# A logsumexp kernel without its check on the sums and without the branch that the check decides

## The chip, the cores and the metric

The kernel runs on one core of a Trainium2 chip. Its engines work side by side, each through its own list of instructions, and wait for each other on semaphores: ScalarE (ACT) computes functions such as exp and Ln, VectorE (DVE) sums, TensorE (PE) multiplies matrices, SyncE (SP) issues the transfers (DMAs) between the chip's main memory and the on-chip memory, and GpSimd (POOL) does nothing here but set constants at the start. The metric is the device time of one execution in microseconds (us).

## The reference

```python
def reference(x, axis):            # x: 32 x 512 x 1024 float32, normally distributed; axis = -1
    x_max = np.max(x, axis=axis, keepdims=True)
    return (x_max.squeeze(axis) + np.log(np.sum(np.exp(x - x_max), axis=axis))).astype(np.float32)
```

For each of 16,384 rows of 1024 numbers it gives the logarithm of the sum of the exponentials. The input has 67.1 MB, the output 64 KB.

## The kernel before

The 16,384 rows are spread over the 128 partitions, 128 rows on each. The kernel computes exp without subtracting the row's maximum first, sums, and takes the Ln. That is right as long as the sums stay in a safe range, so this version looks at the sums afterwards, and a branch leads to a second computation, with the maximum subtracted, where one of them is outside it.

The 128 rows of a partition come in 17 chunks (`CHUNKS`), of 4 to 16 rows at the start and in the middle, and 5, 4, 3, 2, 1, 1, 1, 1 at the end. SP loads each chunk with one DMA into a ring of 51 rows (line 119), and waits before it until the rows that stood there have been used. ACT waits for the chunk's landing. For the first rows of a chunk (second number in `CHUNKS`) it computes exp in place (line 163), and DVE sums them (line 183, or in halves, line 170). For the other rows, all of the last four chunks among them, ACT adds up while it computes exp, by means of its accumulator, which a separate read instruction stores (line 190). The sums of the last four rows go to a tensor of their own, `late`, the others to `sums`.

`take_logs` (line 123) is the Ln of a stretch of rows into `res` (line 127). It is called three times: for 81 rows when the chunk with index 7 (`LN_AT`) comes, for the 43 rows that follow directly behind the last exp, and for the last four rows. SP then waits for the last Ln and issues the output's DMA (line 232).

The check on the sums has these steps. `count` (line 200) compares sums with a lowest and a highest value and adds up how many lie inside, twice per call, on DVE (line 204): once for the 124 sums of `sums`, once for the 4 of `late`, after the last Ln. PE multiplies the counts by `ones` and so adds over the partitions (line 226), DVE adds the four results into one whole number, `n_good` (line 229). SP, ACT and DVE each wait for it, load it into a register (line 236) and branch (line 274): if it is not 2 x 128 x 128, they carry out the second computation (lines 241 to 273), and otherwise jump behind it. In the second computation ACT has 8 x 16 exps and one Ln, DVE 8 maxima, 8 sign changes and an addition, SP 8 loads and a store.

At the end SP waits until all three engines have loaded the register (line 277), clears the semaphores (line 278), takes `known` back to zero (line 279), and waits for the landing of the output, `stored` (line 280), which it takes back too (line 281).

## Time and profile before

| what | value |
|---|---|
| time, median of 3 runs | 165.16 us (165.04 to 165.38) |
| time of the profiled execution | 165.16 us |
| span of the profiled execution | 161.5 us, 171 instructions |
| input and output over the span | 67.18 MB, 416 GB/s on average |
| DVE busy | 122.1 us (76% of the span), of it 111.2 us sums on line 183 |
| ACT busy | 115.1 us (71%), of it 104.4 us exps on line 163 |
| PE busy | 0.2 us |

The span goes from the kernel's first instruction to its last; what the runtime does ahead of it and behind it is not in it, but the time contains some of that. A line of a view that tells of instructions names the source line (L163), the engine, the operation, what is written from what (`ring<-ring`) and how often. SPq, ACTq and DVEq are the engines' sequencers, which wait, branch, load registers and issue DMAs. In the chain that ended last, each piece is what released the next one. In a table of windows a row holds the stretch in us from the span's start, its length, the busy time of PE, weight loads, DVE, ACT and POOL with the number of instructions, the TensorE clock that was granted, the busy share of the DMA engines, and GB/s.

### The profile page before, as it was taken

How to read it: one execution, taken by the hardware profiler on the slowest of the kernel's cores; microseconds unless marked ns; L12 is line 12 of the kernel's file. 1: busy time of each engine (PE TensorE's matmuls, PEld its weight loads, DVE VectorE, ACT ScalarE, POOL GpSimd, SP SyncE). 2: the span in 40 equal slices, each digit the busy share in tenths (PEclk: the TensorE clock that was granted, in tenths of full speed). 3: DMA queues.
4: the chain of work that ended last, by engine and by line, in shares of the span. 5: the costliest groups of instructions: out<-in, count | busy, mean ns of one | idle time of the engine just before them, and what ended most of it. 6: DMA issues, size and time to landing. Idle time of an engine off the chain costs nothing.

```text
span 161.5 us, 171 instructions
## 1 busy us (share of the span) xinstructions
PE 0.2 (0%) x2; PEld 0.1 (0%) x2; DVE 122.1 (76%) x56; ACT 115.1 (71%) x40; POOL 0.2 (0%) x4
## 2 busy tenths in 40 slices
PE   0000000000000000000000000000000000000000
PEld 0000000000000000000000000000000000000000
DVE  0028000003999999999999599999999999999894
ACT  3170005996079960999419993999199999999995
POOL 0000000000000000000000000000000000000000
DMA  7999899979979979979979999999999999999990
GB/s 272 491 487 426 365 426 520 438 341 520 438 341 520 438 341 520 438 341 520 438 309 455 455 455 438 422 422 422 412 429 429 422 440 395 452 402 439 402 396 27
DMA packets 2593, 67.18 MB, mean 416 GB/s; under 512 B 288, under 2 KB 416, under 8 KB 928
## 3 DMA queue, kind: packets, MB, share of 16 engines
q1 hardware_dynamic: 2592, 67.18, 97.2%
q14 instruction: 1, 0.01, 0.0%
HBM read 67.11 MB, written 0.07 MB: 416 GB/s over the span
## 4 chain that ended last, share of the span: by engine, by line
DMA 48%; DVE 30%; ACT 20%; issue 1%; PE 0%; ACTq 0%
DMA ring<-in_x_dram 48%; DVE sums L183 29%; ACT ring L163 17%; ACT ring L190 3%; DVE marks L204 0%; ACT res L127 0%; PE good L226 0%; DVE n_good L229 0%; ACTq L126 0%
## 5 line engine op out<-in xcount | busy, mean ns | idle before, releaser
L183 DVE TENSOR_REDUCE sums<-ring 128x8 f32<-128x8192 f32 (+5 forms) x14 | 111.2, 7994 | 35.6 <-ACT ring L163 35.6
L163 ACT ACTIVATE ring<-ring 128x8192 f32<-128x8192 f32 (+6 forms) x18 | 104.4, 5836 | 43.2 <-DMA ring<-in_x_dram 43.1
L170 DVE CUSTOM_DVE_ANT_0 ring<-ring 128x512 f32<-128x512 f32 x16 | 9.9, 689 | 0.0
L190 ACT ACTIVATE ring<-ring 128x1024 f32<-128x1024 f32 x9 | 9.3, 1044 | 0.0
L150 ACT ACT_TABLE_LOAD x1 | 1.3, 1283 | 1.4 <-PEq L89 1.4
L190 ACT ACTIVATION_READ_ACCUMULATOR ring<-ring 128x1 f32 x9 | 1.6, 173 | 0.0
L170 DVE DVE_READ_ACCUMULATOR2_ANT sums<- 128x1 f32 x16 | 1.4, 85 | 0.0
L149 DVE MEMSET ones<- 128x1 f32 x1 | 0.1, 59 | 1.5 <-PEq L89 1.5
L204 DVE TENSOR_SCALAR_CACHE_REDUCE marks<-late 128x4 f32<-128x4 f32 x2 | 0.3, 190 | 0.9 <-ACT res L127 0.9
L204 DVE TENSOR_SCALAR_CACHE_REDUCE marks<-sums 128x124 f32<-128x124 f32 x2 | 0.5, 309 | 0.0
L127 ACT ACTIVATE res<-sums 128x81 f32<-128x81 f32 (+1 forms) x2 | 0.5, 242 | 0.0
L226 PE MATMUL good<-counts,ones 128*1 128x4 f32 x2 | 0.2, 166 | 160.1 <-DVE marks L204 160.1
L229 DVE TENSOR_REDUCE n_good<-good 1x1 int32<-1x4 f32 x1 | 0.1, 148 | 0.3 <-PE good L226 0.3
L204 DVE DVE_READ_ACCUMULATOR marks<-sums 128x1 f32 x2 | 0.3, 142 | 0.0
L204 DVE DVE_READ_ACCUMULATOR marks<-late 128x1 f32 x2 | 0.3, 163 | 0.0
L127 ACT ACTIVATE res<-late 128x4 f32<-128x4 f32 x1 | 0.2, 173 | 0.0
L226 PEld LDWEIGHTS good<-counts,ones 128*1 128x1 f32 x2 | 0.1, 80 | 160.1 <-DVE marks L204 160.1
L309 POOL MEMSET const-uint8-127<- 128x1 uint8 x1 | 0.1, 102 | 0.0
L309 POOL MEMSET const-bfloat16-1.0<- 128x1 bf16 x1 | 0.1, 101 | 0.0
L309 POOL MEMSET const-float32-0.0<- 128x1 f32 x1 | 0.1, 98 | 0.2 <-issue 0.2
L309 POOL MEMSET const-float32-1.0<- 128x1 f32 x1 | 0.1, 98 | 0.0
## 6 DMA issues: line engine op xcount, KB each, us to landing
ring<-in_x_dram SPq DMA_DIRECT2D x1, 7680.0 KB, 24.4
ring<-in_x_dram SPq DMA_DIRECT2D x1, 7168.0 KB, 28.7
ring<-in_x_dram SPq DMA_DIRECT2D x1, 6656.0 KB, 35.8
ring<-in_x_dram SPq DMA_DIRECT2D x1, 4608.0 KB, 20.3
ring<-in_x_dram SPq DMA_DIRECT2D x2, 2048.0 KB, 16.1
ring<-in_x_dram SPq DMA_DIRECT2D x1, 3584.0 KB, 28.4
ring<-in_x_dram SPq DMA_DIRECT2D x1, 2560.0 KB, 27.3
ring<-in_x_dram SPq DMA_DIRECT2D x4, 512.0 KB, 27.0
```

The lines of the kernel that those rows point to most:

```text
L127: nc.scalar.activation(out=res[:, lo:hi], in_=src, func=Ln).then_inc(act_done, 1)
L149: check(nc.vector.memset(ones, 1.0))
L150: nc.scalar.preload_act_table_set("natural_log_exp_and_others")
L163: nc.scalar.activation(out=ring[:, s + lo : s + hi], in_=ring[:, s + lo : s + hi], func=Exp).then_inc(act_done, 1)
L170: nc.vector.tensor_tensor_reduce(out=ring[:, s + j, : D // 2], in0=ring[:, s + j, : D // 2], in1=ring[:, s + j, D // 2 :], scale=1.0, scal ...
L183: nc.vector.reduce_sum(out=sums[:, row + lo : row + hi], in_=ring[:, s + lo : s + hi], axis=AX).then_inc(dve_done, 1)
L190: nc.scalar.activation(out=ring[:, s + j], in_=ring[:, s + j], func=Exp, accum_out=total(row + j),).then_inc(act_done, 1)
L204: nc.vector.tensor_scalar(out=marks[:, c * NB + at : c * NB + at + n], in0=src, scalar1=bound, scalar2=None, op0=op, op1=Op.add, accum_out ...
L226: check(nc.tensor.matmul(good[:1, :4], lhsT=ones, rhs=counts, start=True, stop=True))
L229: nc.vector.reduce_sum(out=n_good, in_=good[:1, :4], axis=AX).then_inc(known, 1)
L309: nc = _bacc.Bacc("TRN2", target_bir_lowering=False, num_devices=1)
```

## The change

The check on the sums goes, and with it the branch and the second computation: the counts, the matrix product, the number `n_good`, the three register loads, and all semaphores that belong to them. The three calls of `take_logs` and the output's DMA stay, in their order. At the end SP clears the semaphores as soon as it has issued the output's DMA, and waits for the landing after that.

```diff
-    top, low, total_g, res_g = (ring[:, STEP, k * NB : (k + 1) * NB] for k in range(4))
...
-    check(nc.vector.memset(ones, 1.0))
     nc.scalar.preload_act_table_set("natural_log_exp_and_others")
...
-    def count(src, k, at):
-        ...
-    nc.vector.wait_ge(dve_done, dves)
-    nc.vector.wait_ge(act_done, done_before[-1 - LATE][1])
-    count(sums[:, :late_row], 0, 0)
     last_sum = acts
 
     take_logs(logged, late_row, sums[:, logged:late_row], *done_before[-1 - LATE])
     take_logs(late_row, NB, late[:, : NB - late_row], dves, last_sum)
-    nc.vector.wait_ge(act_done, acts)
-    count(late[:, : NB - late_row], 1, late_row)
-    nc.tensor.wait_ge(checked, checks)
-    check(nc.tensor.matmul(good[:1, :4], lhsT=ones, rhs=counts, start=True, stop=True))
-    nc.vector.wait_ge(checked, checks)
-    with nc.allow_low_precision(reason="small whole numbers"):
-        nc.vector.reduce_sum(out=n_good, in_=good[:1, :4], axis=AX).then_inc(known, 1)
-
     nc.sync.wait_ge(act_done, acts)
     nc.sync.dma_start(out=out_v, in_=res).then_inc(stored, 16)
 
-    for engine, reg in ((nc.sync, E.SP), (nc.scalar, E.Activation), (nc.vector, E.DVE)):
-        engine.wait_ge(known, 1)
-        engine.reg_load(deciders[reg], n_good)
-        engine.sem_inc(known, 1)
-
-    with nc.If_ne(deciders, 2 * P * NB):
-        ...
-    nc.end_ifs()
-
-    nc.sync.wait_ge(known, 4)
     nc.sync.sem_clear(range(used[0], used[-1] + 1))
-    nc.sync.sem_inc(known, -4)
     nc.sync.wait_ge(stored, 16)
     nc.sync.sem_inc(stored, -16)
```

## The prediction

> **What bounds the kernel now.** I read the page's chain first, then the end of the span in the timeline, then what ends each wait on the output's path, and last the windows behind the span, because the change touches only what comes after the last sum. The page and its chain:

> ```profile
> span 161.5 us, 171 instructions
> ## 4 chain that ended last, share of the span: by engine, by line
> DMA 48%; DVE 30%; ACT 20%; issue 1%; PE 0%; ACTq 0%
> DMA ring<-in_x_dram 48%; DVE sums L183 29%; ACT ring L163 17%; ACT ring L190 3%; DVE marks L204 0%; ACT res L127 0%; PE good L226 0%; DVE n_good L229 0%; ACTq L126 0%
> ```

> Up to the last exp the bound is the input stream, with exps and sums in step with it. The change leaves all of that alone. It can earn something only where the chain has L204, L226 and L229: after the last Ln. The chain in order of time, its end:

> ```profile
> 155.37 3.02 ACT ring L190 x7
> ...
> 159.48 0.21 ACT res L127 x2
> 159.70 0.02 issue
> 159.72 0.37 DVE marks L204 x4
> 160.09 0.04 issue
> 160.13 0.21 PE good L226 x2
> 160.34 0.02 issue
> 160.36 0.15 DVE n_good L229
> ```

> ACT is done at 159.69 us. From there two strands run side by side: the output's DMA on SP, and the count, matmul, sum, register loads and branch. The timeline, the DMA issues and the answers for tile n_good and line 274 show both:

> ```profile
> 159.71 0.35 SPq L232 DMA_DIRECT2D out_dram<-res  x1
> ```

> ```profile
> out_dram<-res SPq DMA_DIRECT2D x1, 64.0 KB, 1.5
> ```

> ```profile
> L236 SPq TENSOR_LOAD <-n_good x1: 461/461/461, 160.5 to 160.5; - x1
> L236 ACTq TENSOR_LOAD <-n_good x1: 461/461/461, 160.5 to 160.5; - x1
> L236 DVEq TENSOR_LOAD <-n_good x1: 540/540/540, 160.5 to 160.5; - x1
> ```

> ```profile
> L274 SPq COMPARE_BRANCH  x1: 45/45/45, 161.1 to 161.1; - x1
> L274 ACTq COMPARE_BRANCH  x1: 45/45/45, 161.1 to 161.1; - x1
> L274 DVEq COMPARE_BRANCH  x1: 72/72/72, 161.2 to 161.2; - x1
> ```

> The output is issued at 159.71 and its last receipt arrives 1.5 us later (161.26 in the trace's semaphore records). The branches end at 161.1 to 161.2. So the whole check on the sums lies beside the output's flight and sticks out by little. After the branch SP still clears semaphores and updates two more (lines 278, 279, 281, in a row, about 0.08 us apart), and the span ends at 161.45.

> **Behind the span.** The execution took 165.16 us (the median of the runs is the same number), its span 161.45: 3.71 us lie around the span. The trace goes on after it. The windows there:

> ```profile
> 161.50:161.90 0.40, 0.00 (x0) 0.00 (x0) 0.00 (x0) 0.00 (x0) 0.00 (x0) 1.00 0.00 0
> 161.90:162.60 0.70, 0.00 (x0) 0.00 (x0) 0.00 (x0) 0.00 (x0) 0.00 (x0) 1.00 0.05 12
> 162.60:164.20 1.60, 0.00 (x0) 0.00 (x0) 0.00 (x0) 0.00 (x0) 0.00 (x0) 1.00 0.00 0
> 164.20:164.70 0.50, 0.00 (x0) 0.00 (x0) 0.00 (x0) 0.00 (x0) 0.00 (x0) 1.00 0.04 16
> ```

> The last two numbers are the DMA share and GB/s: in a time without kernel work one transfer appears, 12 GB/s for 0.7 us, some 8 KB. In the DMA records it is one 8192-byte packet of the instruction queue, from 161.975 to 162.506, that is 0.87 us after ACT's branch ended. The semaphore records tell the rest. Semaphore 2, which the kernel does not own, is updated at 160.497, which is 0.16 us after PE's last matmul reported (160.336), and then eight more times, at 163.809, .847, .891, .915 up to 164.131. Then some 250 semaphores are cleared until 164.70, and a second such round of semaphore 2 runs from 164.92 to 165.28. I read the rounds as a meeting of the five engines, one after another: PE arrives first, the second arrives at 163.81, and the others, already there, follow within some 0.04 us each. That second engine kept everybody waiting for 2.4 us after SP's end. POOL had nothing to do since 1.4 us, so it is one of the three that branch. Of these ACT skips most: the fallback has 8 x 16 exps and a Ln for it, 129 instructions, against 8 x 2 + 1 on DVE and 8 loads, a store and a few semaphore steps on SP. So I take it that ACT, having jumped, had to fetch its next instructions, and the end of the execution waited for that.

> **The change part by part.**
> Removed on DVE: `ones`' memset (0.06 us at 1.5 us; ACT's first exp waits for data until 7.43, so nothing); the count over 124 sums (158.21 to 158.80, beside the last exp, with nothing queued on DVE that the output needs): nothing. The count over the last 4, the matmul, the sum and the loads of the register run from 159.72 to 161.09, beside the output's flight to 161.26: nothing by themselves. If the output landed sooner than 161.1, they would have been the end; it does not.
> Removed on SP, behind the output's issue: wait for the count, register load, branch, wait for the other two. `sem_clear` now follows the issue directly and is over by about 160.2, hidden by the flight. Left behind the landing: the wait for `stored` and its update, 0.017 us, which reports at 161.453 at present, 0.19 us after the last receipt. It will be at 161.26 + 0.04 = 161.30. **Span: 161.45 - 0.15 = 161.30 us.**
> Both Ln calls and the output's issue stay where they are: the diff does not touch `take_logs`, so no part of the change comes from the Ln.
> Removed behind the span: the three jumps. ACT ends its program at 159.70 and goes straight on, DVE at 158.2. If the fetch after the jump is what the meeting waited for, the last to arrive is SP. In the kernel before the fifth hop, the last of the way forth and so by the order of arrival SP's at the latest, is at 163.915. What SP needs from its last instruction to the meeting is not shown, since it is hidden behind 163.81. Bounds: PE's 0.16 us from one side, and from the other 1.30 us, the time from the end of the fetched packet (162.51) to the late arrival (163.81), which may be plain end-of-program work. I take PE's row, since it alone is an engine that went on without a jump. Then SP arrives at 161.30 + 0.16 = 161.46 in place of 163.915: **2.46 us less, 165.16 - 2.46 = 162.70 us**; with 1.30 it is 162.60, 1.32 us less, 163.84. The span's 0.15 us is contained in both. The meeting can't be earlier than 161.3, so the time goes no lower than about 162.55, and the runs' own scatter (165.04 to 165.38) takes it to 162.45.

> [...] The row: a packet of instructions 0.87 us after the branch, and an engine late by 2.4 us. [...]

> **The rivals.**
> *Only the span shrinks, 165.0 us.* Either the late arrival isn't the jump's doing (the end of any program takes that long on ACT or SP), or the 3.71 us lie ahead of the span: the semaphore records also show a round at -3.82 to -2.39 us. Against the first: PE passes in 0.16 us, and the packet comes just after the branch. Against the second: the closing round ends at 165.28, close to 165.16. If it holds, the price is 165.16 - 0.15 = 165.01. A chance of 0.17.
> *The fetch moves to SP, slower.* [...] If SP, the last to finish, has to fetch at its end, it pays there what the late engine pays now: from 161.105 (branch) to 163.81, 2.70 us, so it arrives at 161.30 + 2.70 = 164.00 in place of 163.915, about 165.25. A second fetch of 0.87 us behind it makes 166.1. It decides against the change from a delay of 2.95 us on (163.915 + 0.33 - 161.30). [...] A chance of 0.06.

> **How the numbers follow.** What a measurement of this kernel can tell from no change is about 0.2%, 0.33 us. The meeting comes early: 0.77, by itself 162.45 to 163.85, likeliest 162.70. Only the span: 0.17, 164.85 to 165.2. Slower: 0.06. All of the first is faster by over 0.2%, all of the second within. To leave out no more than 2 in 10 the range takes in the second case: 162.45 to 165.10.

> **What would show it.** A span of 161.30, with the output's issue at 159.71 and its landing 1.5 us later as before; no L204, L226, L229, L236, L274. Behind the span: no 8 KB of instructions within 1.5 us of ACT's end, and the eight updates of semaphore 2 beginning at 161.5 or before. If the fetch is gone and the meeting still waits until about 163.7, the closing code itself takes that long and the first rival holds. If the meeting comes early and the time stays, the 3.71 us are ahead of the span. If the output lands later or the last exp ends after 159.5, the difference comes from the input stream, and this prediction has missed its place.

## The result, and the profile after

The changed kernel takes 162.59 us (median of 6 runs, 162.49 to 162.74) against 165.16 us (164.62 to 165.41) for the kernel before: a ratio of 0.9846, with a 95% interval of 0.983 to 0.9863. The forecast was 162.70 us, in a range from 162.45 to 165.10. Its profiled execution took 162.59 us, of which the span is 161.27. So 0.18 us of the 2.57 are inside the span, and the rest behind it: what lies around the span (the time less the span) went from 3.71 us to 1.32.

The head of the page, the chain and the chain's end in order of time, after:

```profile
span 161.3 us, 149 instructions
## 4 chain that ended last, share of the span: by engine, by line
DMA 48%; DVE 29%; ACT 20%; issue 1%; ACTq 0%
DMA ring<-in_x_dram 48%; DVE sums L154 29%; ACT ring L134 17%; ACT ring L161 3%; ACT res L107 0%; ACTq L106 0%
```

```profile
159.30 0.15 ACT ring L161
159.45 0.20 ACT res L107 x2
```

Up to the last Ln the chain is what it was; L204, L226 and L229 are gone from it, and nothing has taken their place. Line numbers have shifted (L107 is the Ln of `take_logs`, L176 the output's issue). The timeline's and the DMA issues' lines of the output:

```profile
159.68 0.35 SPq L176 DMA_DIRECT2D out_dram<-res  x1
```

```profile
out_dram<-res SPq DMA_DIRECT2D x1, 64.0 KB, 1.6
```

The windows behind the span, of the kernel after (no PE columns here, since PE has no work):

```profile
161.50:161.90 0.40, 0.00 (x0) 0.00 (x0) 0.00 (x0) 1.00 0.00 0
161.90:162.60 0.70, 0.00 (x0) 0.00 (x0) 0.00 (x0) 1.00 0.00 0
162.60:164.20 1.60, 0.00 (x0) 0.00 (x0) 0.00 (x0) 1.00 0.00 0
```

The 12 GB/s that stood in the second of these windows are gone. The trace's records of semaphore 2, which show where the five engines meet behind the program, in us from the span's start:

| | first (PE) | second | third | fourth | fifth | ninth | second round ends |
|---|---|---|---|---|---|---|---|
| before | 160.497 | 163.809 | 163.847 | 163.891 | 163.915 | 164.131 | 165.279 |
| after | 1.654 | 159.770 | 159.808 | 159.852 | 161.410 | 161.573 | 162.717 |

Read together the rows name the engines. PE, without work in the kernel after, comes at 1.65. The second follows ACT's last Ln (159.66) by 0.11 us, so it is ACT. The fifth follows SP's last instruction (161.268) by 0.14 us, so it is SP, and it is now the one that the others wait for.

### The profile page after: what moved, and what is told of

It is laid out like the page before. It is cut to its first block, busy times and chain, and to the rows that moved or that the text cites. A ratio compares the mean times of both kernels' runs of the same rounds, so it can differ in the third digit from the quotient of the medians.

```text
span 161.3 us, 149 instructions
## 1 busy us (share of the span) xinstructions
DVE 121.0 (75%) x46; ACT 115.0 (71%) x40; POOL 0.2 (0%) x4
## 4 chain that ended last, share of the span: by engine, by line
DMA 48%; DVE 29%; ACT 20%; issue 1%; ACTq 0%
DMA ring<-in_x_dram 48%; DVE sums L154 29%; ACT ring L134 17%; ACT ring L161 3%; ACT res L107 0%; ACTq L106 0%
## 5 line engine op out<-in xcount | busy, mean ns | idle before, releaser
L107 ACT ACTIVATE res<-sums 128x81 f32<-128x81 f32 (+1 forms) x2 | 0.5, 242 | 0.0
L107 ACT ACTIVATE res<-late 128x4 f32<-128x4 f32 x1 | 0.2, 173 | 0.0
```

The source lines that it names most:

```text
L107: nc.scalar.activation(out=res[:, lo:hi], in_=src, func=Ln).then_inc(act_done, 1)
```

## The experiments

In the kernel before, ACT's branch jumps over 128 exps with accumulator and a Ln, its part of the second computation. The theory: ACT's jump over them waits for instructions, and the meeting waits for ACT. The readings are, for each run, the end of ACT's branch, the second update of semaphore 2, the time between them, and the first 8192-byte packet of the instruction queue behind the branch, in us, all from its profiled execution, and then the device time. A time marked * is the median of 4 runs or more, any other is a single run. The kernel before was timed again beside the experiments: 165.05 us with e1 to e4, 164.97 with e5 to e8, 165.22 with e9 to e11, 164.63 with e12; the ratios below are to these runs.

| kernel | branch ends | second update | between | packet | time |
|---|---|---|---|---|---|
| before | 161.105 | 163.809 | 2.70 | 161.975 | 165.16* |
| after | none | 159.770 | | none | 162.59* |
| e1, no branch | none | 160.680 | | none | 162.62* |
| e2, ACT skips 1 exp a step | 161.376 | 161.915 | 0.54 | 162.362 | 163.09* |
| e5, 4 exps a step | 160.833 | 161.377 | 0.54 | 162.059 | 162.73 |
| e6, 8 exps a step | 161.015 | 161.559 | 0.54 | 162.005 | 162.92 |
| e7, 12 exps a step | 161.361 | 164.165 | 2.80 | 162.240 | 165.52 |
| e9, 8 a step, 64 exps added far ahead | 160.811 | 161.354 | 0.54 | 161.797 | 162.71 |
| e12, 12 a step, 64 exps added far ahead | 161.158 | 161.701 | 0.54 | 162.141 | 163.01* |
| e3, ACT alone jumps | 161.604 | 164.179 | 2.58 | 162.476 | 165.02* |
| e4, whole guard, wide exps | 161.253 | 161.462 | 0.21 | 162.887 | 163.05* |
| e8, the same, early clear | 160.927 | 161.131 | 0.20 | 162.579 | 163.01* |

The profiled executions fall into groups by what lies around the span, too: 1.32 to 1.33 us in the kernel after, e1 and e10, where no jump stands at the end; 1.56 in e2, e5, e6, e9 and e12; 3.71 to 3.82 in the kernel before, e3 and e7. (e4 and e8, with 1.56 and 1.54, have another ending, told below.)

**e1: the checks without the branch.**

```diff
-    with nc.If_ne(deciders, 2 * P * NB):
-        ...
-    nc.end_ifs()
```

> The kernel before with the branch and the second computation left out; counts, matrix product, n_good, the three register loads and the wait for all three stay. Theory (ACT's jump over the second computation waits for instructions): no jump, so semaphore 2's second update comes right behind ACT's register load, at about 161.1, and the fifth follows SP's end by 0.14 us as in the kernel after; with SP's end at 161.35 to 161.45 the time is 162.65 to 162.8. Rival A (any taken branch costs it): the same. Rival B (the checks themselves, the loads of n_good from on-chip memory above all, make ACT late): second update still near 163.8, 165.2 us.

It took 162.62 us, a ratio to the kernel before of 0.9856 (0.9839 to 0.9872), and the counts, the matrix product and the sum cost nothing that can be measured (the kernel after takes 162.59). They are still at the end of its chain:

```profile
159.69 0.37 DVE marks L204 x4
160.06 0.04 issue
160.10 0.21 PE good L226 x2
160.31 0.02 issue
160.33 0.15 DVE n_good L229
```

They end at 160.48, while the output lands beside them. One thing this run doesn't show: with no branch to read the registers the three loads are no longer in the trace, so rival B stays open for them. e2 settles it.

**e2: all three jump, ACT over little.**

```diff
-            for j in range(STEP):
+            for j in range(1):
```

> The kernel before with the branch in place, but ACT's part of the second computation cut to one exp per step (8 exps, 1 Ln), so that all three engines still jump, ACT over few instructions; the second computation, never entered with this input, would be incomplete. Theory with distance (the jump's goal lies outside the instructions that ACT holds): about 162.75, the span 161.45 as before, no 8192-byte packet of instructions behind the span. Rival A (any taken branch empties what the engine holds): second update near 163.8, 165.2 us.

The engines load their registers and jump, and ACT is at the meeting after 0.54 us instead of 2.70: neither the loads nor a taken branch as such make the stall. The time, 163.09 us (ratio 0.988, 0.9864 to 0.9897), is 0.34 above the forecast for it. Most of that lies behind the span: 1.56 us around it against 1.32 in the kernel after. ACT is still the last to arrive: the fifth update comes 0.31 us after SP's last instruction, in the kernel after 0.14. And the packet that the theory excluded is there, 0.99 us behind the branch. A packet just behind the branch is therefore no sign of a stall; it comes in both cases, 0.87 to 0.88 us behind the branch in the three kernels that stall and 0.98 us or more behind it in the others.

**e3: ACT alone jumps.**

```diff
-    with nc.If_ne(deciders, 2 * P * NB):
+    with nc.If_ne(deciders_act, 2 * P * NB):
+        ...                                  # 128 exps and a Ln, on ACT alone
```

> The kernel before with a branch on ACT alone, over 128 exps and a Ln; SP and DVE load the register but don't branch and skip nothing. The second computation is cut to ACT's part and would not work. Theory (it is ACT's jump): second update of semaphore 2 near 163.8, time 165.0 to 165.2, an 8192-byte packet behind ACT's branch. Rival C (the jump of SP or DVE): 162.7 us, no packet.

165.02 us, a ratio of 0.9996 (0.9987 to 1.0006): the whole price is back with ACT's jump alone. SP and DVE don't branch here, and as in e1 their loads of the register are not in the trace.

**e4: a whole guard that leaves ACT little to skip.**

```diff
+            nc.vector.tensor_tensor(out=x_g, in0=x_g, op=Op.subtract,
+                in1=top[:, lo:hi].unsqueeze(2).to_broadcast([P, STEP, D]))
-            for j in range(STEP):
-                nc.scalar.activation(out=x_g[:, j], in_=x_g[:, j], func=Exp, bias=..., accum_out=...)
+            nc.scalar.activation(out=x_g, in_=x_g, func=Exp)
+            nc.vector.reduce_sum(out=total_g[:, lo:hi], in_=x_g, axis=AX)
```

> The whole check and a whole second computation, with the work in it moved: DVE takes the maximum, subtracts it from 16 rows at once and sums, ACT has 8 exps over 16 rows and a Ln, so ACT skips 9 instructions in place of 129 exps and Ln with their accumulator reads. Theory with distance: 162.75 us, 2.4 us below the kernel before with the same protection, and within 0.2 us of the kernel after. Rival A: 165.2 us.

163.05 us, a ratio of 0.9878 (0.9862 to 0.9895): the guard stays and 2 us of its 2.5 are gone. Against the kernel after, 0.46 us remain (0.56 between the two profiled executions, 163.15 and 162.59 us). Of the 0.56, 0.18 lie ahead of the output's issue, where the two programs do the same work on the output's path; 0.15 are SP's steps up to its end: SP ends 1.74 us after the output's issue (159.856 to 161.595), in the kernel after 1.59 (159.681 to 161.268); 0.03 lie in the two rounds of the meeting; and 0.20 lie behind them: the execution ends 0.08 us behind the last update of semaphore 2, and 0.12 to 0.13 ahead of it in the kernels before and after. What these 0.20 us are isn't settled. A packet of instructions comes at 162.89, behind the first round of meeting, so they may be a fetch at the very end.

**e5, e6, e7: how far ACT jumps.** The edit of e2 with 4, 8 and 12 in place of 1.

> As the kernel before, ACT's part of the second computation cut to 4 exps per step: ACT jumps over 32 exps with 32 accumulator reads and a Ln, 65 instructions and some waits, an estimated quarter of the original's 257. The time from the end of ACT's branch to semaphore 2's second update was 2.70 us over 16 exps per step and 0.54 over one. Theory of a threshold: below 0.6 us here. Theory of a cost in proportion to the distance: 0.54 + 2.16 x 3/15 = about 1.0 us, time 163.3 to 163.5.

> The same with 8 exps per step: 129 instructions and some waits skipped. Threshold: either below 0.6 us or about 2.6 us from branch to second update, the latter with an 8192-byte packet 0.87 us behind the branch and 165.0 us. Proportion: 0.54 + 2.16 x 7/15 = 1.5 us, about 164 us.

> The same with 12 exps per step: 193 instructions and some waits skipped. Threshold: as for 8, either below 0.6 or about 2.6 us. Proportion: 0.54 + 2.16 x 11/15 = 2.1 us, about 164.6 us.

The time between is 0.54, 0.54 and 2.80 us: a threshold, no proportion. The windows behind the span, first of e6, then of e7, and the branch of each:

```profile
161.90:162.60 0.70, 0.00 (x0) 0.00 (x0) 0.00 (x0) 0.00 (x0) 0.00 (x0) 1.00 0.05 12
...
164.20:165.00 0.80, 0.00 (x0) 0.00 (x0) 0.00 (x0) 0.00 (x0) 0.00 (x0) 1.00 0.00 0
```

```profile
L274 ACTq COMPARE_BRANCH  x1: 45/45/45, 161.0 to 161.0; - x1
```

```profile
161.90:162.60 0.70, 0.00 (x0) 0.00 (x0) 0.00 (x0) 0.00 (x0) 0.00 (x0) 1.00 0.05 12
...
164.20:165.00 0.80, 0.00 (x0) 0.00 (x0) 0.00 (x0) 0.00 (x0) 0.00 (x0) 1.00 0.04 10
```

```profile
L274 ACTq COMPARE_BRANCH  x1: 45/45/45, 161.3 to 161.3; - x1
```

The first packet looks alike in both. What tells them apart is the second one, at 164.6 us in e7 (164.3 in the kernel before, 164.9 in e3, none in e6). The records don't say which engine a packet is for. If ACT waits for the first one, its transfer is only part of the stall: it ends at 162.51 us in the kernel before, 162.99 in e3 and 162.82 in e7, and ACT arrives 1.19 to 1.35 us after that, where 0.11 to 0.15 us lie between its last instruction and its arrival in the kernel after and e1. What fills the rest, no run shows.

**e8: the clear moved ahead of the loads.**

```diff
+    nc.sync.wait_ge(known, 1)
+    nc.sync.sem_clear(range(used[0], used[-1] + 1))
     for engine, reg in ((nc.sync, E.SP), ...
...
     nc.sync.wait_ge(known, 4)
-    nc.sync.sem_clear(range(used[0], used[-1] + 1))
```

> The whole check and the second computation with ACT's exps over 16 rows, as in the run before it, and SP clears the semaphores while the register loads are still to come, before its branch, in place of after it. SP's steps behind the branch then take 0.12 us less, the clear ahead of the load costs it 0.07: SP ends about 0.1 us earlier, 0.1 us above the kernel after. Theory (what is left between this and the kernel after is SP's end): 162.65 to 162.9 us. Rival (the rest is ACT's or DVE's arrival behind the branch, 0.2 to 0.27 us): no change from 163.05 us.

A miss: 163.01 us, as before the edit. SP ends 1.74 us after the output's issue, as in e4. The clear ahead of the load starts at 160.35 and the load at 160.46, so it delays the load, and with it the branch, by 0.11 us, not 0.07, about what the clear had cost behind the branch (0.12). With SP's end where it was, the time can't decide between theory and rival. The records of semaphore 2 speak against the rival: the fifth update follows SP's end by 0.15 us, in e4 and the kernel after by 0.14, so SP is the last to arrive in all three. As in e4, the execution ends behind the last update of semaphore 2 (0.05 us), and that part stays open.

**e9, e12: the same jumps, elsewhere in ACT's program.**

```diff
+        if i == 1:
+            nc.scalar.wait_ge(checked, 1)
+            for k in range(64):
+                nc.scalar.activation(out=pad[:, k : k + 1], in_=ones, func=Exp)
         nc.scalar.wait_ge(landed[i], 16)
```

> The kernel with 8 exps per step in the part skipped, and 64 exps over a single number per partition added to ACT's program ahead of the second chunk, while ACT waits for data (14.8 us idle). The jump is as long as before, but its goal lies 64 instructions further on in ACT's program, where the goal lies with 12 exps per step. Theory of place (what counts is where the goal stands against the blocks that ACT holds): about 2.7 us from branch to second update, 165.0 to 165.5 us. Rival (the length of the jump counts): 0.54 us as with 8 exps per step, 162.9 us.

The 64 instructions take 6.07 us of ACT's idle time, and the jump doesn't stall, against what I had expected of the theory of place. The trace has one new thing, in the DMA queues of the window from 17 to 18.5 us, where one packet of instructions (at 17.77 us) runs among the data's:

```profile
q14 instruction: 1, 0.01, 1.3%
```

The kernel before has no such packet there: its only one in the span comes at 157.22 us. My guess was that with this packet ACT comes to hold the instructions behind the jump; the run doesn't show it, nor does it tell place from length. From the guess followed a test: with 12 exps a step, the length that stalled, and the same 64 instructions ahead, the jump should not stall.

> 12 exps per step in the part skipped, as in the run that stalled for 2.80 us, and the 64 small exps ahead of the second chunk. [...] Theory of place: no stall, 0.54 us from branch to second update, 162.7 to 163.1 us, with a jump as long as the one that stalled. Rival (the jump's length decides, between 139 and 203 instructions): about 2.8 us from branch to second update, 165.2 us.

0.54 us between branch and second update, and 163.01 us (ratio 0.9886, 0.986 to 0.9912). The jump of the same length costs 2.80 us in e7 and 0.54 here, and only 64 instructions far ahead of it differ. So the place of the jump in ACT's program decides, not its length. Against what this place counts, no run shows.

**e10: the jump where ACT has time.** The kernel after, and behind the first chunk's exp:

```diff
+            nc.scalar.reg_load(decider[mybir.EngineType.Activation], flag)
+            with nc.If_ne(decider, 1):
+                ...                          # 128 exps and a Ln
+            nc.end_ifs()
```

> The kernel after, with a jump on ACT over 128 exps and a Ln like that of the kernel before, but at another place: behind the first chunk's exp, where ACT sits idle for 14.8 us until the second chunk lands. Its register comes from a constant that DVE writes. Theory (the jump costs only because nothing covers it): the fetch of 2.6 us is hidden, the span and the second update as in the kernel after, 162.6 us, at most 162.9. Rival (such a jump costs 2.4 us wherever it is, for instance because later blocks come late each time): 165 us.

162.98 us, 0.39 above the kernel after and far from 165: whatever the jump costs ACT here is covered, and the end of the program is as in the kernel after (SP's last instruction to fifth update 0.14 us). The 0.39 us are in the input stream. ACT's waits and its next exp:

```profile
ACT ring L150 <- DMA ring<-in_x_dram: 43.5, 7, 15.3
```

```profile
26.52 13.00 ACT L150 ACTIVATE ring<-ring 128x15360 f32<-128x15360 f32 x1 [15.34 <-DMA ring<-in_x_dram]
```

The second chunk's last receipt comes at 26.49 us, in the kernel after at 25.92, and in all the other runs from 25.49 to 25.95. Two packets of instructions, at 20.09 and 25.21 us, went through the busy DMA engines (a share of 0.93 from 15 to 19.9 us, 1.00 from 20.5 to 25) with the chunk. That they held up its last receipt is possible, but no run isolates it, and e9 and e12, with one such packet each at about 18 us, have it at 25.63 and 25.95. How long ACT stood isn't shown. Between the two packets lie 5.1 us, in the kernels that stall at the end 2.3 to 2.4, so under the stream the stall may well be longer than the 2.6 us that I had expected.

**e11: the second computation carried out.** e4 with another number in the comparison, so that the branch isn't taken.

> The kernel with the whole check and ACT's exps over 16 rows, its branch comparing with another number, so that the second computation is carried out although the sums are in range: its price when it is needed. No theory of the jump is at stake. Estimate: 8 steps one after another, each of a load of 16 rows (8.4 MB at 416 GB/s, 20 us), a maximum, a subtraction and a sum on DVE (16 rows summed take about 17.3 us by line 183, three times 52) and exps (14 us on ACT): 8 x 86 = 690 us behind the first 161, about 850 us.

868.07 us in a single run, close to the estimate, and its parts come out near what was assumed: 17.2 us for each of DVE's three operations, 13.9 for an exp over 16 rows, 22.4 instead of 20 for the wait for a load. That is what an input out of range costs with the guard of e4. What it costs with the second computation of the kernel before was not run.

## Why the prediction was right, point by point

**The span.** Forecast 161.30 us by way of 0.15 less, measured 161.27 in the profiled execution. From the output's issue to SP's end it is 0.15 us less (1.738 to 1.587), as forecast; the other 0.03 us come from the input stream, with the issue at 159.68 in place of 159.71. SP's last instruction follows the output's landing at once (last receipt 161.234, instruction 161.251 to 161.268), and the check on the sums was hidden by the output's flight, as e1 shows alone.

**The late engine is ACT, because of its jump.** e3 and e2 show it from both sides (2.58 and 0.54 us from the branch to the second update), and e7 against e12 (2.80 and 0.54) shows that the place of the jump in ACT's program decides. That what ACT waits for is instructions is argued from this and from the packets, one of them 0.87 to 0.88 us behind the branch and a second one, at 164.3 to 164.9 us, only where ACT stalls; no run shows the wait itself.

**SP's way to the meeting.** I took PE's 0.16 us; it was 0.14. With the fifth update at 161.410 in place of 163.915 that is 2.505 us. The turn of the round, from the fifth to the sixth update, went from 0.097 to 0.044 us, which I had not seen (it is 0.04 in every run where SP arrives last, and 0.10 where SP has to wait for ACT), and the rest of the two rounds is equal to 0.01. Together 2.56 us, and the times differ by 2.57. The choice of PE's row over the 1.30 us rested on one engine and was not more than argued. From SP's end to the last update of the first round there are 0.31 us.

**Where the 3.71 us lie.** Behind the span: the meeting came 2.5 us earlier and the time fell with it, while the round of updates ahead of the span stayed at -3.9 to -2.4 us.

**How much the hit says.** The range took in the early meeting and the rival that only the span shrinks, so the time's lying inside says little. What speaks for the mechanism is the 162.70, 0.11 us above the measured time, and the signs behind the span.

**Two steps of the working were wrong without harm.** The packet behind the branch, on which I leaned, comes without a stall too; ACT was the right engine all the same, for the other reason that the prediction gave, that it skips most. And I counted 129 instructions skipped on ACT; each exp with an accumulator has a read beside it (a row of its own on line 190 of the page before), so it is 257 and some waits. The number served only to say that ACT skips most, which holds. That such a jump stalls or not by where it stands is what e7 and e12 show (2.80 and 0.54 us); what sets the length and the place at which it does, no run shows.

**The rivals.** That only the span would shrink (165.0 us) fell with the meeting's move. That the fetch would move to SP (165.25 and more) did not happen, the trace after has no packet of instructions from the span's start on.

## What to carry to other kernels

What the taken branch at the end of this program cost was hardly seen in the span (161.45 us with it, 161.27 without, while the time fell by 2.57): look in the windows behind it and at when the engines meet, and compare the time with the span. If a guarded second computation is needed, make the part that an engine skips short, first of all on the engine that has most instructions in it (only ACT's part was varied here): moving the work from 128 row-by-row exps to 8 wide ones kept the guard and returned 2 of its 2.5 us. 64 instructions far ahead turned such a stall off (0.54 us in e12 against 2.80 in e7), so a small change in time with no change in the span deserves this look before it is explained by the edit itself.
